# First mixer of a two-layer trunk: two groups of rotation tables, the state products, the gate weights and the head scales put elsewhere

## The chip, the cores and the metric

The kernel runs on one core of a Trainium2 chip. Its engines are TensorE (PE in the profile; its weight loads are PEld), VectorE (DVE), ScalarE (ACT), GpSimd (POOL) and SyncE (SP, which here issues the loads of weights). The metric is the device time of one execution in microseconds (us); lower is better. Three executions of the kernel before took 1027.24, 1029.93 and 1033.87 us, the median is 1029.93.

## The reference, cut to what matters

Two post-norm layers over 512 positions of width 1024; the even one mixes with HGRN2 heads and S5 groups, the odd one with two kinds of attention, and a mixture of 16 SwiGLU experts follows each. The change touches the even mixer alone:

```python
proj = jnp.einsum('bld,df->blf', x, ev_w_in[j])
q_a, f_a, i_a, g_a, u_b = split_cols(proj, [512, 512, 512, 512, 512])
# HGRN2: 4 heads of 128, chunks of 64 positions
f = lb + (1.0 - lb) * jax.nn.sigmoid(f_logit)
...                                    # b = cumsum(log f) in a chunk, decays exp(b), exp(-b)
o = o_intra + jnp.einsum('bhnck,bhnkv->bhncv', q_dec, S_prev)
o = o * lax.rsqrt(jnp.mean(o * o, axis=-1, keepdims=True) + RMS_EPS)
y_a = o * norm_g * jax.nn.silu(gate)
# S5: h_t = a h_{t-1} + B u_t, complex and diagonal, 32 groups of 16 inputs and 64 states
_, _, h_re, h_im = lax.associative_scan(combine, (a_re, a_im, drive_re, drive_im), axis=1)
y = jnp.einsum('blgp,gnp->blgn', h_re, c_re) - jnp.einsum('blgp,gnp->blgn', h_im, c_im)
y = jax.nn.gelu(y + d_skip * u)
z = jnp.einsum('blc,cf->blf', y, w_glu)
y_b = z[..., :512] * jax.nn.sigmoid(z[..., 512:])
mix = jnp.einsum('blf,fd->bld', jnp.concatenate([y_a, y_b], axis=-1), ev_w_out[j])
```

## The kernel before

Nothing is scheduled by a tool: every engine runs its instructions in the order in which the Python code emits them, and waits by semaphores for what it reads or overwrites. `weave(main, side)` interleaves generators: after each `yield` of the main one (a main step, 6 matmuls of 128x512) it lets the side one go on whose count has run out; a side generator that yields n sleeps for n main steps.

A product in full precision is three matmuls with operands split into a high and a low part (`mm3`, L198 to L200). The parts are made by `hilo`: L193 is the cast to the high part on ScalarE, L194 the subtraction that gives the low part on VectorE. Operands live in 13 buffers of 128x2048 (`unit`, named u), which are given out in turn, so a cast can also wait for the last reader of the buffer that it takes over. `tp`, `sd` and `acc` are PSUM tiles.

The first mixer in order of time:

- The projection of u (`tok(c["u"])`, L488). ScalarE copies the result into U (L485). `s5_tables` is woven in: cosines and sines of the rotation, Tc and Ts, built by doubling, eight groups of six VectorE operations (L861 to L866). The last two groups are the two halves of the last doubling.
- The projections of q, f and g as `main`, with four batches of the S5 scan (`s5_batches`) and `glu_prep` as `side`. One batch is: transposes of VT and U (L918, L924) with their ScalarE copies V and ut (L920, L926); products of EP and BB (L933) with ScalarE copies to MM (L938); GpSimd prepares VT and EP of the next batch (L879 to L903); sd from ut and V (L948); on VectorE the rotation of sd by Tc and Ts (L951 to L956), two scans (L958, L959) and the rotation back into H0 (L964) and H1 (L967); on TensorE the state products yp from MM, ut, EP and H (L972, L974); on VectorE their sum into U (L976). `YB` says after how many main steps each part of a batch goes on. `glu_prep` is the Gelu of U (L985, ScalarE) and, one per main step, four blocks fb of transposes (L992) with their `hilo`. Beside the last batch, `hgrn_f` does the gate's scan L540, the exponentials L544 and L545 (ScalarE) and their products L549 and L550 (VectorE) in two halves. The Silu of the g projection is L494. Sigmoid, log, exp, Gelu and Silu need different ScalarE tables; a change of table shows as ACT_TABLE_LOAD.
- `hgrn_main`, woven with the S5 gate product `glu()`: transposes L588, L590, state sums L614, L615, outputs L624, L628, and per block of 128 positions the sums of squares ms (L633). L581 multiplies the gate G by the norm weights ng, on GpSimd, once for all.
- `hgrn_out`, woven with the first half of the output product `wo_k`: the reciprocal roots scale the heads of V (L647), G multiplies them (L648), and L654 transposes the result.

Nothing after the mixer is touched. Line numbers are the profile's of the kernel before; in the changed kernel the same lines stand 2 to 5 further down (L194 is L196, L948 is L953, L974 is L979, L985 is L990).

## Time and profile before

| | us |
|---|---|
| three executions | 1027.24, 1029.93, 1033.87 |
| profiled execution, whole | 1029.0 |
| its span, first to last instruction | 1027.3 |
| PE busy | 852.1 (83%) |
| DVE busy | 789.2 (77%) |
| ACT busy | 562.3 (55%) |
| POOL busy | 308.3 (30%) |

The trace was taken from one execution; 1.7 us of its time lie outside the span. The first mixer ends at about 276 us of the span; the rest, 751 us, is the mixture of experts of the even layer, the odd layer and its mixture. Busy shares are means over stages that are bound by different things, so the time of a stage is read from what its waits end on. The mean granted clock of TensorE is given as a share of its full 2.4 GHz; 0.5 is the lower level, 1.2 GHz.

### The profile page before, as it was taken

How to read it: one execution, taken by the hardware profiler on the slowest of the kernel's cores; microseconds unless marked ns; L12 is line 12 of the kernel's file. 1: busy time of each engine (PE TensorE's matmuls, PEld its weight loads, DVE VectorE, ACT ScalarE, POOL GpSimd, SP SyncE). 2: the span in 40 equal slices, each digit the busy share in tenths (PEclk: the TensorE clock that was granted, in tenths of full speed). 3: DMA queues.
4: the chain of work that ended last, by engine and by line, in shares of the span. 5: the costliest groups of instructions: out<-in, count | busy, mean ns of one | idle time of the engine just before them, and what ended most of it. 6: DMA issues, size and time to landing. Idle time of an engine off the chain costs nothing.

```text
span 1027.3 us, 13161 instructions
## 1 busy us (share of the span) xinstructions
PE 852.1 (83%) x4396; PEld 713.6 (69%) x4396; DVE 789.2 (77%) x1542; ACT 562.3 (55%) x907; POOL 308.3 (30%) x343
## 2 busy tenths in 40 slices
PE   6968888889895789999885599989996689999830
PEld 5857777678784668888663488878785568888720
DVE  6996565656868879999777756888878869999647
ACT  3321334723402588998676245666712478999731
POOL 6357770210100222222221310245630222322203
PEclk9998999889997899999998699999998789999985
DMA  9312010301292879999893452060075869999822
GB/s 285 116 41 81 21 64 10 120 4 42 103 374 81 338 246 334 379 342 387 269 326 105 170 155 41 2 164 1 2 244 216 325 214 314 377 369 363 260 76 115
DMA packets 52875, 192.05 MB, mean 187 GB/s; under 512 B 13492, under 2 KB 15552, under 8 KB 38336
## 3 DMA queue, kind: packets, MB, share of 16 engines
q1 hardware_dynamic: 37344, 156.47, 41.8%
q0 software_dynamic: 13440, 24.17, 8.9%
q10 hardware_dynamic: 2016, 10.49, 2.6%
q8 instruction: 38, 0.62, 0.2%
q14 instruction: 37, 0.30, 0.1%
HBM read 183.20 MB, written 31.98 MB: 209 GB/s over the span
## 4 chain that ended last, share of the span: by engine, by line
PE 33%; issue 14%; DMA 13%; DVE 9%; POOL 5%; ACT 4%; SPq 1%; another core or an unknown queue 1%; ACTq 0%; POOLq 0%; DVEq 0%
DMA yd<-row,r 8%; PE acc L198 7%; PE acc L200 7%; PE acc L199 7%; DMA rx<-in_moe_w_gate_up_dram 2%; DVE u L194 2%; POOL yd L1612 2%; PE tp L207 2%; PE tp L1405 1%; DMA row<-yd 1%; ACT u L193 1%; POOL xg L1569 1%; DMA u<-in_moe_w_down_dram 1%; POOL row L1774 1%; PE sd L199 1%
## 5 line engine op out<-in xcount | busy, mean ns | idle before, releaser
L198 PE MATMUL acc<-u 128*128 128x512 f32 (+1 forms) x712 | 296.8, 417 | 9.9 <-ACT u L193 8.2
L200 PE MATMUL acc<-u 128*128 128x512 f32 (+1 forms) x712 | 282.3, 397 | 9.2 <-DVE u L194 9.2
L199 PE MATMUL acc<-u 128*128 128x512 f32 (+1 forms) x712 | 281.4, 395 | 3.0 <-POOL u L194 1.9
L194 DVE TENSOR_TENSOR u<-u 128x1024 fp32r<-128x1024 f32 x142 | 174.5, 1255 | 31.5 <-ACT u L193 30.3
L193 ACT CAST u<-u 128x1024 fp32r<-128x1024 f32 x150 | 152.7, 1050 | 68.9 <-PE acc L200 50.1
L194 DVE TENSOR_TENSOR u<-rx,u 128x1024 fp32r<-128x1024 f32 x128 | 152.3, 1220 | 29.6 <-ACT u L193 28.4
L200 PEld LDWEIGHTS acc<-u 128*128 128x128 f32 x712 | 141.3, 198 | 39.3 <-DVE u L194 12.2
L198 PEld LDWEIGHTS acc<-u 128*128 128x128 f32 x712 | 143.7, 202 | 33.4 <-ACT u L193 10.4
L199 PEld LDWEIGHTS acc<-u 128*128 128x128 f32 x712 | 142.5, 200 | 25.5 <-DVE u L194 3.5
L193 ACT CAST u<-rx 128x1024 fp32r<-128x1024 f32 x128 | 129.5, 1048 | 3.9 <-issue 1.3
L1612 POOL DMA_INDIRECT yd<-row,r x37 | 58.6, 1583 | 238.2 <-ACT row L1611 193.4
L193 ACT CAST u<-tp 128x512 fp32r<-128x512 f32 x102 | 60.1, 606 | 78.0 <-PE tp L207 67.1
L194 DVE TENSOR_TENSOR u<-tp,u 128x512 fp32r<-128x512 f32 x102 | 67.8, 698 | 19.0 <-ACT u L193 18.9
L1569 POOL DMA_INDIRECT xg<-x1d,r x41 | 47.3, 1153 | 77.0 <-PE tp L207 67.1
L207 PE MATMUL tp<-idf,xg 128*128 128x128 f32 x312 | 49.6, 299 | 16.4 <-DMA xg<-x1d,r 9.8
L207 PEld LDWEIGHTS tp<-idf,xg 128*128 128x128 f32 x312 | 46.7, 208 | 21.5 <-issue 10.0
L198 PE MATMUL acc<-u,ht 128*128 128x512 f32 x148 | 58.4, 395 | 4.0 <-ACT ht L193 4.0
L1395 POOL TENSOR_SCALAR P<-P,st 128x256 f32<-128x256 f32 (+3 forms) x32 | 35.0, 1094 | 87.5 <-DVE st L1371 52.3
L199 PE MATMUL acc<-u,ht 128*128 128x512 f32 x148 | 57.7, 390 | 0.0
L200 PE MATMUL acc<-u,ht 128*128 128x512 f32 x148 | 57.6, 389 | 0.0
L1611 ACT ACTIVATE row<-acc,r 128x512 f32<-128x512 f32 x74 | 47.7, 686 | 9.9 <-PE acc L200 9.9
L1113 ACT COPY u<-tp 128x512 f32<-128x512 f32 x16 | 9.4, 587 | 66.5 <-PE tp L1112 56.4
(394 smaller groups left out, 1443.5 us busy)
## 6 DMA issues: line engine op xcount, KB each, us to landing
rx<-in_moe_w_gate_up_dram SPq DMA_DIRECT2D x48, 1024.0 KB, 11.7
u<-in_moe_w_gate_up_dram SPq DMA_DIRECT2D x24, 1024.0 KB, 17.4
u<-in_moe_w_down_dram SPq DMA_DIRECT2D x19, 1024.0 KB, 15.4
rx<-in_moe_w_down_dram SPq DMA_DIRECT2D x16, 1024.0 KB, 13.2
u<-in_ev_w_in_dram SPq DMA_DIRECT2D x10, 1024.0 KB, 5.7
u<-in_ev_w_out_dram SPq DMA_DIRECT2D x4, 1024.0 KB, 4.9
x1d<-row POOLq DMA_DIRECT2D x8, 512.0 KB, 6.4
yd<-row ACTq DMA_DIRECT2D x8, 512.0 KB, 2.7
```

The source lines that it names most:

```text
L193: self.nc.scalar.copy(hi, src)
L194: (self.nc.gpsimd if pool else self.nc.vector).tensor_sub(lo, src, hi)
L198: nc.tensor.matmul(ps, ah, bh, start=start, stop=False)
L199: nc.tensor.matmul(ps, ah, bl, start=False, stop=False)
L200: nc.tensor.matmul(ps, al, bh, start=False, stop=stop)
L207: self.nc.tensor.transpose(tp[:, blk(j)], src[:, s], self.idf)
L1395: nc.gpsimd.tensor_scalar(P[:, 1, :W], P[:, 1, :W], st[:, 5, 1:2], None, op0=MUL)
L1405: nc.tensor.transpose(tp[:, blk(2 * b + x)], P[:, x, blk(b0 + b)], self.idf)
L1569: nc.gpsimd.indirect_dma_start(out=xg, out_offset=None, in_=self.x1d, in_offset=bass.IndirectOffsetOnAxis(ap=self.toki[:, s:s + 1], axis=0 ...
L1611: nc.scalar.activation(ys[:, blk(c, 512)], yp[c], AF.Copy, scale=self.gate[:, s:s + 1])
L1612: return lambda: self.scattered(s, nc.gpsimd.indirect_dma_start(out=self.yd, out_offset=bass.IndirectOffsetOnAxis(ap=self.toki[:, s:s + 1] ...
L1774: nc.gpsimd.tensor_mul(r[:, hi], r[:, hi], g[:, hi])
```

## The change

Four edits of the first mixer, all in the order or the engine of operations; the arithmetic is the same.

1. Of the eight groups of `s5_tables` six are woven into the projection of u, and the last two (12 VectorE operations) are emitted inside the first batch, after the preparation of the next batch and ahead of L948.
2. `YB` goes from 1, 2, 2, 3, 2 to 1, 2, 2, 5, 0: the state products stand two main steps later, and the next batch starts right behind them. The last batch yields 3 behind them, so that `glu_prep` comes later too.
3. L581, one GpSimd product of 128x2048, goes; `hgrn_main` multiplies G by ng in four VectorE operations of 128x512, each behind the sum of squares of its block.
4. L647, four VectorE products of 128x512, become 16 ScalarE copies of 128x128 with a scale per partition.

```diff
--- before.py
+++ after.py
@@ -1,4 +1,5 @@
 from contextlib import ExitStack
+from itertools import islice
 
 import concourse.bass as bass
 import concourse.tile as tile
@@ -32,9 +33,10 @@
 AHEAD = 6
 HGY = 7
 PSP = ()
-YB = 1, 2, 2, 3, 2
+YB = 1, 2, 2, 5, 0
 NTMP = 64
 NPREP = 8
+NTAB = 6
 NFIRST = 4
 SPT = 1
 PRE = 3
@@ -485,7 +487,8 @@
                 nc.scalar.copy(U[:, :, j].rearrange("c r g n -> c g r n"),
                                a.rearrange("c (g r n) -> c g r n", g=2, n=16))
             tabs = self.s5_tables()
-            weave(self.tok(c["u"], put_u, lambda j: slice(j, None, 4)), tabs)
+            early = islice(tabs, NTAB)
+            weave(self.tok(c["u"], put_u, lambda j: slice(j, None, 4)), early)
 
             def main():
                 yield from self.feat(c["q"], lambda j, a: nc.scalar.activation(Q[:, j, :], a, AF.Silu))
@@ -497,7 +500,7 @@
                 run_all(decay)
 
             def side():
-                yield from self.s5_batches(U)
+                yield from self.s5_batches(U, tabs)
                 yield from self.glu_prep(U)
             weave(main(), side())
             e5.close()
@@ -578,7 +581,6 @@
             z = hg.tile([128, 128], F32, name=f"S{h}", bufs=3)
             nc.gpsimd.memset(z, 0.0)
             S.append(z)
-        nc.gpsimd.tensor_mul(G, G, ng.unsqueeze(1).to_broadcast([128, NT, 512]))
         ms = self.ms = hg.tile([128, NT, 4], F32, name="ms")
 
         def front(tt):
@@ -631,6 +633,7 @@
             sq = hg.tile([128, 512], F32, name="sq", bufs=2)
             nc.scalar.activation(sq, po, AF.Square)
             nc.vector.reduce_sum(ms[:, tt, :], sq.rearrange("p (h v) -> p h v", h=4), axis=AX.X)
+            nc.vector.tensor_mul(G[:, tt, :], G[:, tt, :], ng)
             yield 1
 
     def hgrn_out_prep(self, O):
@@ -643,8 +646,8 @@
     def hgrn_out(self, O, G):
         nc = self.nc
         for tt in range(NT):
-            o4 = O[:, tt, :].rearrange("p (h v) -> p h v", h=4)
-            nc.vector.tensor_mul(o4, o4, self.rsm[:, tt, :].unsqueeze(2).to_broadcast([128, 4, 128]))
+            for h in range(4):
+                nc.scalar.activation(O[:, tt, blk(h)], O[:, tt, blk(h)], AF.Copy, scale=self.rsm[:, tt, h:h + 1])
             nc.vector.tensor_mul(O[:, tt, :], O[:, tt, :], G[:, tt, :])
         self.dump("ya", O)
         yield HGY
@@ -902,7 +905,7 @@
             G.tensor_tensor(EP[0][sl, :, 1:5, g, :], t1[sl], t2[sl], op=SUB)
             G.tensor_scalar(EP[1][sl, :, 1:5, g, :], u1[sl], -1.0, None, op0=MUL)
 
-    def s5_batches(self, U):
+    def s5_batches(self, U, tabs):
         nc, s5, I = self.nc, self.s5, self.I
         Vv = nc.vector
         big = lambda nm: s5.tile([128, 4, 128], F32, name=nm)
@@ -910,7 +913,6 @@
         f2 = lambda a: a.rearrange("p r c -> p (r c)")
         for q in range(4):
             ps, EP = slice(4 * q, 4 * q + 4), self.EPs[q % 2]
-            Tc, Ts = self.Tc[:, ps], self.Ts[:, ps]
             Vm = []
             for i in range(2):
                 tp = self.tp()
@@ -939,6 +941,9 @@
             if q < 3:
                 self.s5_inputs(q + 1)
                 self.s5_outputs(q + 1)
+
+            run_all(tabs)
+            Tc, Ts = self.Tc[:, ps], self.Ts[:, ps]
             yield YB[0]
 
             dps = []
@@ -974,7 +979,7 @@
                     nc.tensor.matmul(o, self.H[i][:, r, :], EP[i][:, r, 1:5].rearrange("p k g n -> p (k g n)"),
                                      start=False, stop=i == 1)
             Vv.tensor_add(Y[:, ps], Y[:, ps], yp.rearrange("c (r l f) -> c r l f", r=4, l=4))
-            yield YB[4]
+            yield YB[4] if q < 3 else 3
         self.Y = Y
 
     def glu_prep(self, U):
```

The order on VectorE around the end of the projection of u, before. L863 to L866 are the last table operations; u there are the tables Tc and Ts, p the rotations that they are doubled by, g scratch.

```order
L863 TENSOR_TENSOR u<-g_808,g_809 128x16x32
L864 TENSOR_TENSOR g_808<-u,p_202 128x512
L865 TENSOR_TENSOR g_809<-u,p_201 128x512
L866 TENSOR_TENSOR u<-g_808,g_809 128x16x32
L194 TENSOR_TENSOR u<-u 128x1024 x3
L951 TENSOR_TENSOR g_1063<-sd,u 128x512
L952 TENSOR_TENSOR h_1065<-sd,u 128x512
```

In the changed kernel the three splits of q's first operands stand behind the sixth group:

```order
L867 TENSOR_TENSOR g_808<-u,p_200 128x512
L868 TENSOR_TENSOR g_809<-u,p_199 128x512
L869 TENSOR_TENSOR u<-g_808,g_809 128x16x32
L196 TENSOR_TENSOR u<-u 128x1024 x3
L864 TENSOR_TENSOR g_808<-u,p_201 128x512
L865 TENSOR_TENSOR g_809<-u,p_202 128x512
```

and the last operations ahead of the first batch's rotation are these:

```order
L866 TENSOR_TENSOR u<-g_808,g_809 128x16x32
L867 TENSOR_TENSOR g_808<-u,p_202 128x512
L868 TENSOR_TENSOR g_809<-u,p_201 128x512
L869 TENSOR_TENSOR u<-g_808,g_809 128x16x32
L956 TENSOR_TENSOR g_1063<-sd,u 128x512
L957 TENSOR_TENSOR h_1065<-sd,u 128x512
```

So the three L194 moved ahead of the last two groups, and these stand between them and L956, which is L951 before.

TensorE between the state products of the first batch and the second batch, before. L198 to L200 are the main steps' matmuls, of which 42 stand between L948 and the first L972, and 12 between the last L974 and L918:

```order
L972 MATMUL sd<-MM,ut 128x128
L974 MATMUL sd<-EP_147,H_155 128x128
L974 MATMUL sd<-EP_148,H_156 128x128
L198 MATMUL acc<-u 128x512
L199 MATMUL acc<-u 128x512
L200 MATMUL acc<-u 128x512
```

and now, with 54 matmuls between L953 and the first L977:

```order
L977 MATMUL sd<-MM,ut 128x128
L979 MATMUL sd<-EP_147,H_155 128x128
L979 MATMUL sd<-EP_148,H_156 128x128
L920 MATMUL tp<-idf,VT_151 128x128 x4
L920 MATMUL tp<-idf,VT_152 128x128 x4
L926 MATMUL tp<-idf,U 128x128 x4
```

The two main steps that stood behind the state products stand ahead of them, and the transposes of the next batch follow at once.

ScalarE from the first exponentials to the first Silu, before (L193 with tp is the high part of a Gelu block fb):

```order
L544 ACT_TABLE_LOAD
L544 ACTIVATE u<-u 128x1024
L545 ACTIVATE u<-u 128x1024
L193 CAST u<-u 128x1024
L985 ACT_TABLE_LOAD
L985 ACTIVATE u<-U 128x16x2x16 x4
L544 ACT_TABLE_LOAD
L544 ACTIVATE u<-u 128x1024
L545 ACTIVATE u<-u 128x1024
L193 CAST u<-tp 128x4x128 x2
L193 CAST u<-u 128x1024
L494 ACT_TABLE_LOAD
```

and now:

```order
L547 ACT_TABLE_LOAD
L547 ACTIVATE u<-u 128x1024
L548 ACTIVATE u<-u 128x1024
L195 CAST u<-u 128x1024
L547 ACTIVATE u<-u 128x1024
L548 ACTIVATE u<-u 128x1024
L990 ACT_TABLE_LOAD
L990 ACTIVATE u<-U 128x16x2x16 x4
L195 CAST u<-u 128x1024
L497 ACT_TABLE_LOAD
L497 ACTIVATE G<-acc 128x512 x2
L195 CAST u<-tp 128x4x128
```

The second pair of exponentials moved ahead of the Gelu, with one table load less, and the casts of the Gelu's blocks now stand between the Silus of G (two of the four ahead of the first cast).

## Rows read from the trace of the kernel before

**Rows 1.** Stages by window: us; PE, PEld, DVE, ACT, POOL busy; clock; DMA.

```profile
60.00:104.00 44.00, 31.36 (x153) 26.71 (x153) 32.26 (x39) 9.37 (x15) 24.02 (x33) 0.88 0.21 71
104.00:158.20 54.20, 47.78 (x258) 40.84 (x257) 32.31 (x35) 17.94 (x27) 40.87 (x54) 0.94 0.12 40
158.20:210.90 52.70, 41.58 (x200) 33.12 (x199) 35.22 (x40) 29.87 (x37) 12.37 (x19) 0.89 0.19 65
210.90:276.00 65.10, 60.97 (x371) 51.32 (x370) 42.17 (x110) 23.57 (x36) 1.87 (x3) 0.98 0.07 20
```

**Rows 2.** Timeline of PE, batches 0 to 3: start, length, idle before in brackets.

```profile
65.81 0.50 PE L198 MATMUL acc<-u 128*128 128x512 f32 x1 [1.62 <-ACT U L485]
...
76.58 1.12 PE L924 MATMUL tp<-idf,U 128*128 128x128 f32 x4 [8.24 <-ACT V L920]
...
97.23 0.73 PE L974 MATMUL sd<-EP,H 128*128 128x128 f32 x2 [2.16 <-DVE H L967]
...
101.11 0.48 PE L198 MATMUL acc<-u 128*128 128x512 f32 x1
...
103.94 1.04 PE L918 MATMUL tp<-idf,VT 128*128 128x128 f32 x8
...
158.19 1.03 PE L918 MATMUL tp<-idf,VT 128*128 128x128 f32 x8
...
165.16 0.48 PE L198 MATMUL acc<-u 128*128 128x512 f32 x1
```

**Rows 3.** The window of batch 0's state products, columns as in rows 1.

```profile
94.00:101.20 7.20, 4.46 (x23) 4.27 (x24) 4.24 (x5) 0.00 (x0) 2.89 (x3) 0.76 0.23 61
```

**Rows 4.** Timeline of DVE: tables, splits, chains of batches 0 and 1.

```profile
60.84 0.77 DVE L861 TENSOR_TENSOR g<-u,p 128x512 f32<-128x512 f32 x1
...
65.65 0.69 DVE L861 TENSOR_TENSOR g<-u,p 128x512 f32<-128x512 f32 x1
...
69.75 0.69 DVE L861 TENSOR_TENSOR g<-u,p 128x512 f32<-128x512 f32 x1
...
73.74 3.55 DVE L194 TENSOR_TENSOR u<-u 128x1024 fp32r<-128x1024 f32 x3
...
83.34 0.69 DVE L951 TENSOR_TENSOR g<-sd,u 128x512 f32<-128x512 f32 x1 [6.05 <-PE sd L948]
...
96.41 0.77 DVE L967 TENSOR_TENSOR H<-g,g 128x508 f32<-128x508 f32 x1
...
123.60 0.69 DVE L967 TENSOR_TENSOR H<-g,g 128x508 f32<-128x508 f32 x1
```

**Rows 5.** Timeline of ACT: the cast ahead of batch 0's copies.

```profile
74.99 1.05 ACT L193 CAST u<-u 128x1024 fp32r<-128x1024 f32 x1 [7.77 <-DVE u L194]
```

**Rows 6.** Timeline of ACT behind the Gelu.

```profile
189.41 1.28 ACT L544 ACT_TABLE_LOAD   x1
...
192.76 1.96 ACT L193 CAST u<-tp 128x512 fp32r<-128x512 f32 x2
...
198.37 1.04 ACT L193 CAST u<-u 128x1024 fp32r<-128x1024 f32 x1 [3.65 <-PE tp L992]
```

**Rows 7.** Timeline of DVE: the last split of the S5 gate's weights.

```profile
205.54 4.70 DVE L194 TENSOR_TENSOR u<-u 128x1024 fp32r<-128x1024 f32 x1 [0.76 <-ACT u L193]
```

**Rows 8.** Timeline of POOL: the gate product.

```profile
204.65 4.51 POOL L581 TENSOR_TENSOR G<-G,ng 128x2048 f32<-128x2048 f32 x1 [6.28 <-ACT G L494]
```

**Rows 9.** Timeline of PE: the last wait ahead of L588.

```profile
210.30 0.79 PE L200 MATMUL acc<-u 128*128 128x512 f32 x1 [4.01 <-DVE u L194]
```

**Rows 10.** Timeline of DVE at the end of the mixer.

```profile
262.00 3.49 DVE L194 TENSOR_TENSOR u<-u 128x1024 fp32r<-128x1024 f32 x3
...
270.79 1.22 DVE L194 TENSOR_TENSOR u<-u 128x1024 fp32r<-128x1024 f32 x1
```

**Rows 11.** Timeline of PE at the end of the mixer.

```profile
272.66 1.25 PE L654 MATMUL tp<-idf,V 128*128 128x128 f32 x8 [2.98 <-DVE u L194]
```

**Rows 12.** Groups by shape, ACT: a later stage's 128x128; xcount | busy, mean ns.

```profile
L1381 ACT ACTIVATE P<-acc,st 128x128 f32<-128x128 f32 x16 | 5.7, 366 | 3.5 <-DVE st L1375 1.6 <-DVE st L1373 1.5 <-DVE st L1372 0.4
```

## Prediction

> **What bounds the kernel now.** I read the windows by stage first, then the timelines of the engines that wait there. In the four stages that the change touches [rows 1], 60 to 276 us, TensorE is busy 31.4 of 44.0, 47.8 of 54.2, 41.6 of 52.7 and 61.0 of 65.1 us; so up to 34 us of the mixer are TensorE's waiting, while VectorE has room in each (32 of 44, 32 of 54, 35 of 53, 42 of 65). Everything behind the mixer is the same code, waits for the mixer's end and should shift as a block.
>
> Where TensorE waits [rows 2]: 1.62 us for the copies into U and 8.24 us for the copies of V (at 65.81 and 76.58), then for H1 behind the scan (2.16 us at 97.23). The 8.24 us come from ScalarE: its queue stands at a cast that takes over a buffer whose last reader is L194 [rows 5], and L194 stands on VectorE behind the last two groups of tables, from 65.65 to 73.74 [rows 4]. Nothing of batch 0 needs these tables before L951, and VectorE then idles 6.05 us for L948 [rows 4]. The state products of batch 0 run at a granted clock of 0.76 as the mean of their window [rows 3], so partly at the lower level, 1.2 GHz, after the waits on H. Batches 1 and 2 repeat the wait on H; from L918 to L918 they take (158.19 - 103.94)/2 = 27.1 us each [rows 2]. Ahead of the HGRN stage TensorE waits 4.01 us [rows 9] for a split that took 4.70 us [rows 7] while GpSimd ran L581 [rows 8]; the same split takes 3.55/3 = 1.2 us elsewhere [rows 4].
>
> **Term A, to L918 of batch 1.** Rates first. The twelve main matmuls between 101.11 and 103.94 took 2.83 us [rows 2]: 0.236 us each, and 54 of them 12.7 us. From L918 to the end of L948 batch 3 took 165.16 - 158.19 = 7.0 us [rows 2], with no long wait in it. In the changed order the cast ahead of U's copies takes a buffer that is read earlier, so the 1.62 us go, and L918 starts at 67.3 - 1.6 = 65.7; L948 ends at 72.7, the 54 matmuls at 85.4. VectorE: three splits from 65.65 to 69.2, then the two late groups. A group took 69.75 - 65.65 = 4.10 us with GpSimd idle and 65.65 - 60.84 = 4.81 us with GpSimd at work [rows 4]. GpSimd starts the next batch's preparation some 2 us behind L918, so I take 4.81: the tables end at 78.8 (77.4 by the other). The chain from L951 to the end of L967 took 97.18 - 83.34 = 13.8 us [rows 4], beside GpSimd all the way: H1 stands at 92.6. VectorE is then the bound of batch 0, and TensorE waits some 7 us at the state products. From H1 to the next main matmul it took 101.11 - 97.23 = 3.9 us [rows 2], at the low clock; after so long a wait I keep that: L918 of batch 1 at 96.5 instead of 103.94. A = 7.4. With the short table time, a chain one us shorter (GpSimd ends before it does) and the full clock it would be 11; with everything 1.5 us longer, 6.
>
> **Term B, batches 1 and 2.** H1 of batch 1 ended at 123.60 + 0.69 = 124.29 [rows 4], 20.35 us behind its L918, a time that VectorE's own chain sets. Two more main steps ahead of the state products fill the wait: 7.0 + 12.7 = 19.7, then 0.6 us of wait. One such wait is shorter than each that now stands there (2.16 in batch 0), so I take the full clock for what follows, half of 3.9, 2.0 us. The next L918 comes at 20.35 + 2.0 = 22.4 instead of 27.1 us: 4.7 us per batch, B = 9.4. If the clock falls all the same it is 24.3, and B = 5.6; if waits inside the chain shrink too, 10. GpSimd needs about 20 us of such a batch (40.9 us in two batches [rows 1]), so it fits in 22.4, with little to spare.
>
> **Term C, batch 3 to L588.** Before: 210.9 - 158.2 = 52.7 us [rows 1]. The Gelu was done at 189.41 [rows 6], 31.2 us behind L918. In the new order the second pair of exponentials runs ahead of it: 192.76 - 189.41 - 1.28 = 2.1 us [rows 6], its table load left out. The Gelu ends at 33.3. TensorE is at 22.4 behind the state products and has 30 matmuls, 7.1 us, until the first Gelu block: 29.5, so a new wait of up to 3.8 us there. Behind the Gelu ScalarE's queue sets the pace: before, it took from 198.37 [rows 6] to 205.54 [rows 7], 7.2 us, for two casts of weights, a table load, four Silus and two casts of blocks; now there are four casts of blocks, 1.96 us more [rows 6]: 33.3 + 9.1 = 42.4. Then the last split, 1.2 us, since L581 is gone, and the last matmuls: L588 at about 43.8. C = 52.7 - 43.8 = 8.9. If the chain of batch 3 comes later, or the casts wait for TensorE's transposes, which wait for the splits of the blocks ahead, C falls to 5.5; with the faster ends it is 10.5.
>
> **Term D, the end of the mixer.** Four products of G by ng, 0.69 us each (the 128x512 products of [rows 4]), come to VectorE. Three stand in a stage where VectorE idles 22.9 of 65.1 us [rows 1], behind the sums of squares, where it waits for TensorE; should that cover be gone, they cost 2.1 us. The fourth stands ahead of the roots: 0.7 us on the path. Off the path come the four L647: the eight products took from 262.00 + 3.49 to 270.79, 5.3 us [rows 10]. ScalarE's 16 scales are bounded by 128x128 activations of 0.366 us [rows 12], 5.9 us in all, from about 262.7 to 268.6; the last L648 ends at 269.3, where before it ended at 270.8. The second L654, which waited till 272.66 [rows 11], comes 1 to 2 us earlier: D = 1.3.
>
> **The sum.** 7.4 + 9.4 + 8.9 + 1.3 = 27.0 us. The profiled execution took 1029.0, the median is 1029.9, so the two bases differ by 0.9; 1002.0 on the one, 1002.9 on the other. I say 1002.
>
> **Rivals.** One: TensorE stays low. After each wait on H the state products run at 1.2 GHz as now, in batches 1 and 2 too (B = 5.6), and batch 3 loses to its queues (C = 5.5, A = 6, D = 1): 18 us, 1011. For it speaks that rows 3 show the clock low after 2.2 us of waiting; against it, that the waits get shorter in batches 1 and 2.
>
> Two: GpSimd and VectorE shut each other out. The late tables have been put beside GpSimd's preparation of batch 1. If each of the 12 operations had to let one GpSimd operation through, with a mean of 24.02/33 = 0.73 us [rows 1], they would take 12 x (0.69 + 0.73) = 17.0 us, not 9.6; H1 comes 7.4 us later, A is nothing, and the time is 1009.5. The split of 4.70 us beside L581's 4.51 [rows 7, 8] speaks for it, the group of 4.81 us beside a busy GpSimd [rows 4] against it. The Trainium skill, page "SBUF — State Buffer", section "Who interferes with whom", has this as a rule: a VectorE operation with two inputs in SBUF and a GpSimd operation that reads SBUF share a port pair, and the second one blocks fully until the first is done. By that rule the late tables are put in the worse of two places; the trace agrees for the one long GpSimd operation and shows a sixth more time, not a double one, for many short ones.
>
> Three: the gain is not kept. The stages after the mixer, or the longer ScalarE queue, give most of it back: the mixer's end is then no path, and the time is 1020 to 1030. Against it: nothing that follows starts before the mixer's output.
>
> Four, slower: the low clock outlasts a wait. TensorE now waits some 7 us at H of batch 0 and 3.8 us at the Gelu. If the granted clock fell at the Gelu and stayed at 1.2 GHz in the HGRN stage, its 61.0 us of matmuls [rows 1] would take up to 61 us more; from 27 us more, 45% of them, the change is slower, with all of them it is 1063, at two thirds 1043. Against it: the low stretch of [rows 3] ended within 4 us of steady matmuls, and the stage now runs at 0.98.
>
> **How the numbers follow.** The forecast (994 to 1008): 0.68. TensorE low, 1011: 0.13. Shut out, 1009.5: 0.10. Not kept: 0.06. Slower: 0.03. About 1%, 10 us, is what a measurement of this kernel can tell from no change. The first three rivals of the list split so that all of the first two and the forecast are faster by more than that, 0.91; the third lies within it, 0.06; the last is slower, 0.03. The fast ends of the terms (11, 10, 10.5, 2) sum to 33.5, 996, and the executions before lie up to 4 us from their median, so the low end is 994; the high end takes in rivals one and two, 1012.
>
> **What would show it.** In the changed profile: L918 of batch 0 at 65 to 66 with no wait over 1 us to its L948; VectorE without a break from the splits to H1 at 91 to 94; a TensorE wait for H1 of 5 to 8 us in batch 0 and under 1 us in batches 1 and 2; L918 every 22 to 23 us at full clock; a wait of 3 to 4 us at the Gelu's first block, no split of weights over 1.5 us, L588 some 44 us behind batch 3's L918; the second L654 without its 2.98 us; the stage from 276 on as long as before. I am wrong if VectorE's chain grows beyond 14 us, if the clock stays low through whole batches, or if the last stage changes.

## The result, and the profile after

The changed kernel took 1005.46 us as the median of 4 executions (1002.60 to 1008.00); beside it the kernel before took 1031.05 (1027.24 to 1033.87). The ratio is 0.974, with an interval from 0.9705 to 0.9776. A later set of executions of the same two kernels gave 0.971 (0.9685 to 0.9735). Predicted were 1002 and a range from 994 to 1012. The profiled execution has a span of 1001.9 us, 25.4 less than before.

The stages by window, cut at the first transposes of batches 1 and 3, at L590 (L588 before) and at the mixer's end; the columns are those of [rows 1]:

```profile
60.00:97.70 37.70, 29.44 (x153) 25.61 (x152) 34.45 (x39) 8.74 (x14) 31.12 (x33) 0.91 0.20 65
97.70:143.25 45.55, 44.00 (x258) 37.62 (x258) 32.74 (x35) 18.44 (x28) 41.49 (x54) 1.00 0.18 63
143.25:187.20 43.95, 39.32 (x200) 31.29 (x199) 32.78 (x41) 28.15 (x35) 8.62 (x19) 0.96 0.24 78
187.20:252.30 65.10, 62.50 (x383) 52.29 (x383) 44.49 (x112) 29.76 (x53) 3.65 (x4) 1.00 0.11 35
```

TensorE waited some 34 us in [rows 1]; now it is idle 8.3, 1.6, 4.6 and 2.6 us, 17 in all, and half of that is in batch 0. The rows of TensorE that answer to [rows 2, 9, 11]:

```profile
66.75 0.66 PE L926 MATMUL tp<-idf,U 128*128 128x128 f32 x4 [0.24 <-ACT V L922]
...
91.30 0.79 PE L979 MATMUL sd<-EP,H 128*128 128x128 f32 x2 [6.17 <-DVE H L969]
...
93.95 0.80 PE L979 MATMUL sd<-EP,H 128*128 128x128 f32 x2 [1.86 <-DVE H L972]
...
97.74 1.04 PE L920 MATMUL tp<-idf,VT 128*128 128x128 f32 x8
...
118.16 0.49 PE L979 MATMUL sd<-EP,H 128*128 128x128 f32 x2 [0.48 <-DVE H L972]
...
120.50 1.04 PE L920 MATMUL tp<-idf,VT 128*128 128x128 f32 x8
...
174.52 0.33 PE L997 MATMUL tp<-idf,u 128*128 128x128 f32 x1 [1.40 <-ACT u L990]
...
186.98 0.50 PE L202 MATMUL acc<-u 128*128 128x512 f32 x1 [0.63 <-DVE u L196]
...
187.32 0.60 PE L590 MATMUL tp<-idf,F 128*128 128x128 f32 x4
...
246.37 1.25 PE L657 MATMUL tp<-idf,V 128*128 128x128 f32 x8 [0.96 <-DVE u L196]
```

The 8.24 us for the copies of V are 0.24 us now. Where TensorE waited twice for H in every batch it waits once, 0.48 us, in batches 1 and 2, and L920 comes every 22.76 us (120.50 - 97.74) instead of 27.1. In batch 0 the wait grew to 6.17 and 1.86 us. The 4.01 us ahead of L588 and the 2.98 us at the second transposes of the end are 0.63 and 0.96.

The granted clock of TensorE, ahead of the state products of batch 0, through them and behind them, and last behind the Gelu's first block (columns as above):

```profile
84.70:90.50 5.80, 0.44 (x3) 0.21 (x2) 5.80 (x6) 0.00 (x0) 5.76 (x6) 0.97 0.00 0
90.50:97.70 7.20, 4.54 (x22) 4.25 (x23) 4.46 (x6) 0.00 (x0) 3.09 (x4) 0.55 0.20 46
97.70:117.00 19.30, 19.00 (x106) 16.04 (x106) 13.31 (x15) 10.04 (x15) 16.88 (x24) 1.00 0.10 39
176.21:178.91 2.70, 2.70 (x7) 2.02 (x8) 2.07 (x4) 2.67 (x4) 2.17 (x7) 0.50 0.00 0
```

Through the state products of batch 0 it is 0.55, so mostly the lower level of 1.2 GHz; through batches 1 and 2 it is full (1.00 from 97.70 to 143.25). Behind the Gelu's first block it is at the lower level again for 2.7 us: six main matmuls start 0.42 to 0.57 us apart there, where those ahead of the Gelu start 0.23 apart. VectorE, the rows that answer to [rows 4, 7]:

```profile
65.63 4.55 DVE L196 TENSOR_TENSOR u<-u 128x1024 fp32r<-128x1024 f32 x3
...
70.11 1.09 DVE L864 TENSOR_TENSOR g<-u,p 128x512 f32<-128x512 f32 x1
...
80.83 0.69 DVE L956 TENSOR_TENSOR g<-sd,u 128x512 f32<-128x512 f32 x1
...
93.13 0.77 DVE L972 TENSOR_TENSOR H<-g,g 128x508 f32<-128x508 f32 x1
...
185.72 1.21 DVE L196 TENSOR_TENSOR u<-u 128x1024 fp32r<-128x1024 f32 x1
```

It works without a break from the splits to H1 at 93.90, and each part is longer or shorter than it was: the three splits 4.5 us (3.55 before), the two late groups 80.83 - 70.11 = 10.7 (8.1), the chain 13.1 (13.8). ScalarE, around the Gelu and at the end:

```profile
173.83 2.19 ACT L990 ACTIVATE u<-U 128x512 f32<-128x512 f32 x4
...
237.84 4.80 ACT L650 ACTIVATE V<-V,rqy 128x128 f32<-128x128 f32 x16 [0.91 <-DVE rqy L281]
```

The Gelu ends at 176.0, 32.8 us behind L920 of batch 3; the sixteen scales take 4.80 us, one every 0.30.

From the same marks in both traces the four terms are:

| term | marks | before | after | gain | predicted |
|---|---|---|---|---|---|
| A | start of batch 1's first transposes | 103.94 | 97.74 | 6.2 | 7.4 |
| B | from there to those of batch 3 | 54.25 | 45.51 | 8.7 | 9.4 |
| C | from there to L588 | 52.70 | 44.07 | 8.6 | 8.9 |
| D | from there to the second L654 | 61.77 | 59.05 | 2.7 | 1.3 |
| rest | from there to the end of the span | 754.6 | 755.5 | -0.9 | 0 |

They sum to 25.4, the difference of the spans.

### The profile page after: what moved, and what is told of

It is laid out like the page before. It is cut to its first block, busy times and chain, and to the rows that moved or that the text cites. A ratio compares the mean times of both kernels' runs of the same rounds, so it can differ in the third digit from the quotient of the medians.

```text
span 1001.9 us, 13169 instructions
## 1 busy us (share of the span) xinstructions
PE 845.2 (84%) x4396; PEld 707.5 (71%) x4396; DVE 789.1 (79%) x1542; ACT 566.4 (57%) x922; POOL 311.9 (31%) x342
## 3 DMA queue, kind: packets, MB, share of 16 engines
q1 hardware_dynamic: 37344, 156.47, 42.5%
## 4 chain that ended last, share of the span: by engine, by line
PE 47%; issue 15%; DVE 14%; DMA 12%; ACT 5%; POOL 5%; another core or an unknown queue 1%; ACTq 0%; SPq 0%; POOLq 0%; DVEq 0%
PE acc L200 10%; PE acc L202 10%; PE acc L201 10%; DMA yd<-row,r 8%; PE tp L209 2%; DVE u L196 2%; POOL yd L1617 2%; ACT u L195 1%; DMA xg<-x1d,r 1%; PE tp L1410 1%; POOL xg L1574 1%; DMA row<-yd 1%; PE sd L201 1%; PE sd L200 1%; POOL row L1779 1%
## 5 line engine op out<-in xcount | busy, mean ns | idle before, releaser
L200 PE MATMUL acc<-u 128*128 128x512 f32 (+1 forms) x712 | 296.5, 416 | 6.9 <-ACT u L195 6.9
L196 DVE TENSOR_TENSOR u<-u 128x1024 fp32r<-128x1024 f32 x142 | 172.2, 1241 | 27.0 <-ACT u L195 25.9
L195 ACT CAST u<-u 128x1024 fp32r<-128x1024 f32 x150 | 152.9, 1051 | 41.4 <-PE acc L202 36.6
L196 DVE TENSOR_TENSOR u<-rx,u 128x1024 fp32r<-128x1024 f32 x128 | 152.3, 1220 | 28.9 <-ACT u L195 27.8
L200 PEld LDWEIGHTS acc<-u 128*128 128x128 f32 x712 | 143.8, 202 | 29.9 <-ACT u L195 8.7
L200 PE MATMUL acc<-u,ht 128*128 128x512 f32 x148 | 58.5, 395 | 4.0 <-ACT ht L195 4.0
```

The source lines that it names most:

```text
L195: self.nc.scalar.copy(hi, src)
L196: (self.nc.gpsimd if pool else self.nc.vector).tensor_sub(lo, src, hi)
L200: nc.tensor.matmul(ps, ah, bh, start=start, stop=False)
```

## The experiments

Theory: TensorE's waits for the scan are what the mixer lost, the new places of the state products take most of them away, and what is left in batch 0 is VectorE's chain, stretched by GpSimd beside it. Rivals: the late tables or the gate product carry the gain; the wait in batch 0 comes from something else.

All kernels below but one are compared with the kernel before on the same chip. In the table b0, b1, b2 are the times from one batch's first transposes to the next one's, C and D those above; b0 has no part of the 1.62 us wait ahead of the first transposes, which only the kernel before and u_tabs have.

| kernel | ratio to before | interval | b0 | b1 | b2 | C | D |
|---|---|---|---|---|---|---|---|
| before | 1 | | 36.6 | 27.1 | 27.1 | 52.7 | 61.8 |
| changed | 0.974 | 0.9705 to 0.9776 | 32.3 | 22.8 | 22.8 | 44.1 | 59.1 |
| changed, again (base5) | 0.971 | 0.9685 to 0.9735 | 33.0 | 23.1 | 22.8 | 44.1 | 59.0 |
| u_tabs | 0.976 | 0.9722 to 0.9798 | 32.0 | 22.8 | 22.8 | 44.1 | 59.1 |
| u_yb | 0.9903 | 0.9874 to 0.9931 | 35.0 | 27.1 | 27.1 | 49.5 | 60.1 |
| u_gate | 0.9751 | 0.9718 to 0.9784 | 32.2 | 22.8 | 22.7 | 45.1 | 58.6 |
| u_scale | 0.9777 | 0.9737 to 0.9817 | 32.9 | 23.2 | 22.8 | 44.1 | 61.0 |
| a_tabs | 0.9987 | 0.9962 to 1.0011 | 36.1 | 27.1 | 25.5 | 53.5 | 62.7 |
| x_hold | 0.9736 | 0.9701 to 0.9772 | 31.8 | 22.8 | 22.8 | 44.1 | 59.0 |
| v_qtab | 0.9695 | 0.9651 to 0.9739 | 24.8 | 23.1 | 23.1 | 44.1 | 59.1 |
| v_qtab5, the same kernel | 0.9642 | 0.9617 to 0.9667 | 26.0 | 23.3 | 23.1 | 44.1 | 59.0 |
| v_qhold | 0.9662 | 0.963 to 0.9695 | 24.5 | 24.0 | 23.1 | 44.1 | 59.1 |
| v_act | 0.9712 | 0.9684 to 0.9741 | 25.1 | 23.4 | 23.3 | 44.5 | 59.0 |

The changed kernel stands in the table twice, and its own b0 and b1 differ by 0.8 and 0.3 us between two executions: a stage's time from one trace tells about a microsecond there. C and D repeat to 0.1 us wherever an edit leaves them alone.

### The tables: undone (u_tabs) and alone (a_tabs)

```diff
-NTAB = 6
+NTAB = 8
```

> The changed kernel with all eight groups of tables early again (NTAB 8), the rest kept. Theory, both edits work on the same wait of batch 0: the copies of V come late again, and L920 of batch 0 to L953 shifts by some 11 us, but the 54 matmuls and the chain to H1 then end nearly together (H1 at 97 as in the kernel before), so L920 of batch 1 comes at 99.4 instead of 97.7 and the whole is 1.5 to 2.5 us above the changed kernel, 1006 to 1008. Rival, the terms of the prediction add up: term A (6.2 us measured) belongs to the tables, and the time is 1011 to 1012.

Measured: 1006.07 us, ratio 0.976, so about 2 us above the changed kernel's 0.974, with intervals that overlap: the timing alone can't tell the two apart. TensorE's timeline in u_tabs:

```profile
64.70 0.50 PE L200 MATMUL acc<-u 128*128 128x512 f32 x1 [1.62 <-ACT U L487]
...
75.51 1.12 PE L926 MATMUL tp<-idf,U 128*128 128x128 f32 x4 [8.28 <-ACT V L922]
...
95.84 0.49 PE L979 MATMUL sd<-EP,H 128*128 128x128 f32 x2 [0.40 <-DVE H L972]
```

The old waits of 1.62 and 8.28 us are back, but the state products then find H1 after 0.40 us. This trace is already 1.1 us ahead at the first of these waits (64.70, where [rows 2] have 65.81), so the starts of batch 1 can't be compared as they stand. Counted with the wait, b0 takes 31.97 + 1.62 = 33.59 us here and 32.26 in the changed kernel: the late tables are worth 1.3 us (0.6 against base5's b0), under the theory's 1.5 to 2.5. As the theory had it, late tables and later state products spend themselves on one wait.

The other way round, the kernel before with the tables alone:

```diff
+NTAB = 6
-weave(self.tok(c["u"], put_u, lambda j: slice(j, None, 4)), tabs)
+weave(self.tok(c["u"], put_u, lambda j: slice(j, None, 4)), islice(tabs, NTAB))
...
+            run_all(tabs)
+            Tc, Ts = self.Tc[:, ps], self.Ts[:, ps]
             yield YB[0]
```

> The kernel before with the late tables alone. Theory: L918 of batch 0 at 65.5, H1 at 93.9 as in the changed kernel, L918 of batch 1 twelve matmuls behind the state products at 100.5 instead of 103.9; all else as before: 3.4 us below the kernel before. With the run with all tables early this shows whether the gains of the two edits add: alone 3.4, on top of the new YB some 2. Rival, they add: 6 us below.

Measured: 1029.43 us, ratio 0.9987 (0.9962 to 1.0011): no gain that the timing can tell, and the expected 3.4 us lie just inside the interval. In the trace b0 is 0.5 us shorter, and the 1.62 us ahead of it are gone: 2.1 us, less than expected. TensorE's timeline in a_tabs:

```profile
89.16 0.80 PE L978 MATMUL sd<-EP,H 128*128 128x128 f32 x2 [7.96 <-DVE H L968]
...
91.81 0.79 PE L978 MATMUL sd<-EP,H 128*128 128x128 f32 x2 [1.85 <-DVE H L971]
```

The wait for V's copies became a wait for H: 7.96 + 1.85 us, where the kernel before waits 0.62 and 2.16 there. VectorE is the bound of batch 0 either way. Batch 2 is 1.6 us shorter here than in the kernel before (25.5 and 27.1), which the tables don't explain: its waits for H are 1.31 and 1.63 us, much as there (1.26 and 1.63), but the clock stayed at 1.00 behind them (window 147.00 to 149.30), where the kernel before has 0.56 (151.45 to 155.33). C and D are 0.8 and 0.9 us longer, so nothing of this shows in the whole.

### The later state products undone (u_yb)

```diff
-YB = 1, 2, 2, 5, 0
+YB = 1, 2, 2, 3, 2
...
-            yield YB[4] if q < 3 else 3
+            yield YB[4]
```

> The changed kernel with the old YB (1, 2, 2, 3, 2), so state products two main steps earlier, Gelu ahead of the second exponentials; late tables, gate weights and scales as in the changed kernel. Theory: batches 1 and 2 take 27.1 us each again (8.7 in all), L920 of batch 1 comes at 100.5 (2.8 more), batch 3 to L590 takes 49 to 50 instead of 44 (the 4.7 us split stays short): 16 to 18 us above the changed kernel, 1021 to 1023. Rival, the late tables and the gate weights carry the gain: under 8 us above.

Measured: 1020.85 us, ratio 0.9903. That is 16.8 us above the changed kernel's ratio (0.0163 of 1031), as expected. TensorE's timeline in u_yb:

```profile
117.53 0.49 PE L979 MATMUL sd<-EP,H 128*128 128x128 f32 x2 [1.29 <-DVE H L969]
...
119.64 0.79 PE L979 MATMUL sd<-EP,H 128*128 128x128 f32 x2 [1.63 <-DVE H L972]
...
202.39 0.79 PE L202 MATMUL acc<-u 128*128 128x512 f32 x1 [0.43 <-DVE u L196]
```

The two waits for H of 1.29 and 1.63 us are back, and so are the 27.1 us. By stages: b0 2.8, b1 and b2 8.8, C 5.4, D 1.0 us. So one of the change's four edits, the new YB with the order of the Gelu that comes with it, carries most of the gain; the rival falls. What the later state products and the later Gelu are worth each, no run separates.

### The gate product and the head scales undone (u_gate, u_scale)

```diff
+        nc.gpsimd.tensor_mul(G, G, ng.unsqueeze(1).to_broadcast([128, NT, 512]))
...
-            nc.vector.tensor_mul(G[:, tt, :], G[:, tt, :], ng)
```

> The changed kernel with the gate product on GpSimd again (L581 of the kernel before), the four VectorE products by ng taken out. Theory: L581 starts behind the last Silu of G, beside the last splits of the Gelu blocks and of the S5 gate's weights; the last split takes 4 to 5 us again, TensorE waits 3 to 4 us ahead of L590 and its first transposes run at the low clock; the mixer's end gains 0.7 us back: 3 to 4.5 us above the changed kernel. Rival, ScalarE's queue sets L590 and the split is hidden: under 1 us.

Measured: 1006.32 us, ratio 0.9751, about 1 us above the changed kernel and not told apart from it. The expectation was wrong. The timelines of GpSimd, VectorE and TensorE in u_gate around the last split:

```profile
181.49 4.61 POOL L584 TENSOR_TENSOR G<-G,ng 128x2048 f32<-128x2048 f32 x1 [3.83 <-ACT G L497]
```

```profile
185.00 2.18 DVE L196 TENSOR_TENSOR u<-u 128x1024 fp32r<-128x1024 f32 x1
```

```profile
187.24 0.50 PE L202 MATMUL acc<-u 128*128 128x512 f32 x1 [1.58 <-DVE u L196]
```

The product takes 4.61 us, much as before (4.51), but the last split beside it 2.18 and not 4.70: in the new order most of the product is over when the last split comes; they overlap for 1.1 us (185.00 to 186.10), where [rows 7, 8] show 3.6 (205.54 to 209.16). In both kernels the split ends 1.08 us behind the product's end (187.18 - 186.10 and 210.24 - 209.16), and by itself it takes 1.2: so it got next to nothing done while the product ran. TensorE waits 1.58 us instead of 0.63, C is 1.0 us longer and D 0.5 us shorter. In the old order the same product costs much more: u_yb, without it, waits 0.43 us ahead of its L590, and a_tabs, with it, this by its timeline of TensorE:

```profile
204.94 0.79 PE L202 MATMUL acc<-u 128*128 128x512 f32 x1 [4.01 <-DVE u L196]
```

So what the product cost was a matter of where it stood, and the new order had moved the splits away from it before it was taken out.

```diff
-            for h in range(4):
-                nc.scalar.activation(O[:, tt, blk(h)], O[:, tt, blk(h)], AF.Copy, scale=self.rsm[:, tt, h:h + 1])
+            o4 = O[:, tt, :].rearrange("p (h v) -> p h v", h=4)
+            nc.vector.tensor_mul(o4, o4, self.rsm[:, tt, :].unsqueeze(2).to_broadcast([128, 4, 128]))
```

> The changed kernel with the head scales on VectorE again (four products of 128x512 instead of 16 ScalarE copies). Theory: eight products behind the three splits instead of four, so the second group of transposes at the mixer's end comes 1 to 2 us later. Rival, that end is set by ScalarE's casts of the transposed blocks: no difference, under 0.3 us.

Measured: 1008.01 us, ratio 0.9777, some 4 us above the changed kernel with overlapping intervals; in the trace D is 61.01 - 59.05 = 1.96 us longer. TensorE's timeline at the second transposes of the end in u_scale:

```profile
247.78 1.71 PE L657 MATMUL tp<-idf,V 128*128 128x128 f32 x8 [2.93 <-DVE u L196]
```

The wait of 2.93 us is that of [rows 11], 2.98. The theory holds, at its upper end.

### GpSimd beside VectorE (x_hold, x_noprep)

```diff
             run_all(tabs)
+            if q == 0:
+                nc.gpsimd.tensor_copy(s5.tile([128, 4], F32, name="hold"), self.Ts[:, 0:4, 127])
             if q < 3:
                 self.s5_inputs(q + 1)
                 self.s5_outputs(q + 1)
```

> The changed kernel with one small GpSimd copy of a column of the finished table Ts ahead of the preparation of batch 1, so that GpSimd starts it behind the late tables instead of beside them. Theory, contention with GpSimd stretched the splits and the late tables (4.55 and 10.7 us): they take 3.6 to 4.2 and 8.2 to 8.6 us, the chain to H1 13 to 14 us as it is, H1 comes 2 to 3 us earlier and L920 of batch 1 too: 2 to 3 us below the changed kernel. Rival, the operations are slow for another reason (the clock of the engine, waits on each other): 10.7 us still, and GpSimd late with EP for batch 1: 0 to 4 us above.

Measured: 1003.53 us, ratio 0.9736; not told apart from the changed kernel. VectorE, from the first late table operation to L956 (L958 here) to H1:

```profile
68.43 1.09 DVE L864 TENSOR_TENSOR g<-u,p 128x512 f32<-128x512 f32 x1
...
77.12 0.69 DVE L958 TENSOR_TENSOR g<-sd,u 128x512 f32<-128x512 f32 x1
...
90.49 1.09 DVE L974 TENSOR_TENSOR H<-g,g 128x508 f32<-128x508 f32 x1
```

The tables take 8.7 us instead of 10.7, nearly the 8.2 to 8.6 expected, but the splits still take 4.5 and the chain takes 14.5 instead of 13.1: H1 comes 27.8 us behind the first transposes instead of 28.4. So GpSimd's preparation cost VectorE much the same time wherever the two met. The expectation failed in the splits, which run beside two GpSimd operations that stand ahead of the held one, and in the chain, which it took as full of contention already.

```diff
-            if q < 3:
+            if 0 < q < 3:
                 self.s5_inputs(q + 1)
                 self.s5_outputs(q + 1)
...
-            ps, EP = slice(4 * q, 4 * q + 4), self.EPs[q % 2]
+            ps, EP = slice(4 * q, 4 * q + 4), self.EPs[0 if q == 1 else q % 2]
```

> The changed kernel with GpSimd's preparation of batch 1 left out (batch 1 works with batch 0's VT and EP; batch 2's preparation stays). It asks only what VectorE takes in batch 0 without GpSimd beside it. Theory, contention is the whole stretch and holding GpSimd back only moved it: tables 8.2 to 8.4 us, the chain from L956 to H1 11 to 11.5 us instead of 13.1, H1 some 22.5 to 23.5 us behind L920 of batch 0 instead of 28.4 (the first splits, which run beside the two GpSimd operations that stay, still 4.5). Rival, holding gained little because the chain of batch 0 is slow by itself: H1 at 26 or later.

Measured in one execution, read for batch 0 alone; its whole time of 1009.84 us says nothing on the question, since batch 1 then waits for GpSimd's EP (b1 27.8 us). VectorE's timeline in x_noprep, the same three places:

```profile
69.43 1.09 DVE L864 TENSOR_TENSOR g<-u,p 128x512 f32<-128x512 f32 x1
...
78.11 0.69 DVE L956 TENSOR_TENSOR g<-sd,u 128x512 f32<-128x512 f32 x1
...
88.31 0.69 DVE L972 TENSOR_TENSOR H<-g,g 128x508 f32<-128x508 f32 x1
```

Tables 8.7 us (the first of them still beside the two GpSimd operations that stay), chain 10.9, H1 24.2 us behind the first transposes at 64.83: 4.2 us earlier than in the changed kernel. The parts came within 0.3 us of what was expected; the sum in the expectation was too low by a slip (its own parts give 23.7 to 24.4, not 22.5 to 23.5), and 24.2 is well under the rival's 26. So of the 28.4 us that VectorE takes to H1, 4.2 are GpSimd's preparation, and the other 24.2 are VectorE's own work but for the 1 us by which the two GpSimd operations that stay stretch the splits (4.5 us, 3.55 in [rows 4]). Holding GpSimd back could not bring much, and less work for VectorE ahead of H1 could.

### A version that beats both: the last doubling cut by batches (v_qtab, v_qtab5)

Batch q uses four of the sixteen rows of Tc and Ts. So the last doubling can be done for these rows in each batch, where VectorE idles some 5.4 us ahead of L956 in batches 1 to 3:

```diff
             run_all(tabs)
+            self.s5_last(q)
...
+    def s5_last(self, q):
+        ps, o, n_ = slice(4 * q, 4 * q + 4), slice(0, 64), slice(64, 128)
+        cb, sb = [e[:, ps].unsqueeze(2).to_broadcast([128, 4, 64]) for e in self.e[6]]
+        ...                                  # the six operations of a group, 128x256 each
```

> The changed kernel with the last doubling of the tables (12 operations of 128x512) cut into the four rows of each batch: 6 operations of 128x256 in each batch, where the 12 stood in batch 0. The same values. Theory, batch 0 is bound by VectorE and batches 1 to 3 have VectorE idle for some 5.4 us ahead of L956: H1 of batch 0 at 87 to 89 instead of 93.9, L920 of batch 1 at 90 to 92 instead of 97.7; batches 1 and 2 lose up to 1.5 us each because GpSimd, slowed by the new operations beside it, hands over EP with 0.8 us to spare now: 3 to 7 us below the changed kernel, 998 to 1002. Rival, the wait at batch 0 is set by the clock or by GpSimd: no gain.

Measured: 998.39 us, ratio 0.9695. TensorE's timeline in v_qtab, the state products of batches 0 and 1:

```profile
87.27 0.49 PE L995 MATMUL sd<-EP,H 128*128 128x128 f32 x2 [2.17 <-DVE H L988]
...
110.41 0.49 PE L995 MATMUL sd<-EP,H 128*128 128x128 f32 x2 [0.88 <-DVE H L988]
```

The wait of batch 0 fell from 6.17 + 1.86 to 0.18 + 2.17 us, b0 from 32.3 to 24.8 us; b1 and b2 lost 0.3 to 0.4 us each, to a wait for H1 of 0.9 instead of 0.5 us, and not to GpSimd's EP. Both kernels once more, on one chip:

> The kernel with the last doubling cut by batches once more, beside the changed kernel on the same chip: 6 to 7 us below it, as its trace gave (mixer shorter by 6.8 us from L920 of batch 0 to the end). Rival, the stages behind give a part of it back: 3 us or less.

> The changed kernel itself on the same chip as the three before: 0.974 of the kernel before, 25 to 28 us below it.

Measured: 996.34 us, ratio 0.9642 (0.9617 to 0.9667), and the changed kernel 1002.81, ratio 0.971 (0.9685 to 0.9735). The changed kernel is 30 us below the kernel before here, where 25 to 28 were expected. The intervals don't touch: 6.5 us less than the changed kernel, so nearly all of the 6.8 us that the mixer's trace gave arrives at the end.

### Two additions to it (v_qhold, v_act)

```diff
             self.s5_last(q)
+            if q == 0:
+                nc.gpsimd.tensor_copy(s5.tile([128, 4], F32, name="hold"), self.Ts[:, 0:4, 127])
```

> The kernel with the last doubling cut by batches, and GpSimd held back in batch 0 until that batch's part of the tables is done. Theory: splits and the six operations of batch 0 take 2 us less, TensorE's wait for H1 in batch 0 goes from 2.2 to under 0.6 us: 1 to 2 us below the kernel with the cut alone, 996.5 to 997.5 if that takes 998.4. Rival, GpSimd then hands EP of batch 1 over too late (17.4 us from 71 on, wanted at some 89.5) and runs beside the whole chain: no gain or up to 2 us above.

Measured: 997.17 us, ratio 0.9662, not told apart from v_qtab. The rival came true; TensorE's timeline in v_qhold:

```profile
86.03 0.49 PE L997 MATMUL sd<-EP,H 128*128 128x128 f32 x2 [2.32 <-DVE H L990]
...
91.66 1.72 PE L950 MATMUL tp<-EP,BB 128*32 128x128 f32 x14 [0.58 <-POOL EP L921]
```

The wait for H1 is still 2.32 us, and the products of EP now wait 0.58 us for GpSimd.

```diff
-                G.tensor_copy(self.VT[i][sl, :, 3, g, :], self.Bb[i][sl, 4 * q:4 * q + 4, :])
+                (nc.scalar.copy if q else G.tensor_copy)(self.VT[i][sl, :, 3, g, :], self.Bb[i][sl, 4 * q:4 * q + 4, :])
...
-            G.tensor_copy(EP[0][sl, :, 0, g, :], self.C[0][sl, 4 * q:4 * q + 4, :])
-            G.tensor_scalar(EP[1][sl, :, 0, g, :], self.C[1][sl, 4 * q:4 * q + 4, :], -1.0, None, op0=MUL)
+            nc.scalar.copy(...), nc.scalar.mul(...)         # for q > 0, ahead of the power products
```

> The kernel with the last doubling cut by batches, and the plain copies of VT and EP for batches 1 to 3 (8 operations per batch of 64x64 elements, that need no power products) moved from GpSimd to ScalarE. Theory, every GpSimd operation with an input in SBUF stretches VectorE's chain beside it: H1 comes 0.6 to 0.9 us earlier per batch, the waits of 2.2, 0.9 and 0.8 us shrink to 1.4, 0.3 and 0.3: 1 to 2 us below the kernel with the cut alone. Rival, the 128x256 products are what hurts and the copies lie beside nothing: within 0.5 us.

Measured: 1004.00 us, ratio 0.9712: 7.7 us above v_qtab5 on the same chip, where a gain of 1 to 2 or nothing was expected. Neither theory foresaw it. The mixer is not the place: from the first transposes of batch 0 to the second group of the end it takes 239.85 - 64.50 = 175.4 us, in the two traces of v_qtab 174.1 and 175.5. The loss lies behind it. TensorE at the first gathered rows of the mixture of experts, in v_act and in v_qtab5, by their timelines:

```profile
306.81 1.95 PE L209 MATMUL tp<-idf,xg 128*128 128x128 f32 x8 [8.23 <-DMA xg<-x1d,r]
```

```profile
302.38 1.95 PE L209 MATMUL tp<-idf,xg 128*128 128x128 f32 x8 [4.90 <-DMA xg<-x1d,r]
```

Counted from the second transposes of the mixer's end this is 67.0 and 63.6 us: 3.3 of 7.1 us by which the rest of the span is longer (763.95 and 756.84) are lost at a transfer, the gather from x1d. GpSimd begins it only 0.3 us later in v_act (at 300.09, 60.2 us behind those transposes; at 298.74, 60.0 us, in v_qtab5), so the loss is in the gather itself: its first rows reach TensorE 6.7 us behind its start instead of 3.6. But the eight copies are not shown to be the cause: x_noprep, which has none of them, waits 8.20 us for the same gather, and every other trace 4.73 to 4.91. Most of the other 3.8 us come in the second mixture: from its last products of the routing tile r to its last gathered rows it takes 168.5 us in v_act, 165.4 in v_qtab5, and 169.0 in a_tabs, again without the copies. So v_act is slower by more than its interval, and why stays open.

## Why the prediction was right, and where its terms were off

**Term A** was 7.4 and came as 6.2. L918 at 65.7 (65.48), L948's end and the bound by VectorE came as written; the step that was mis-sized is VectorE's time to H1, 92.6 predicted and 93.90 measured. The three splits were taken at 3.5 us and took 4.5, the late groups at 9.6 and took 10.7, the chain at 13.8 and took 13.1: GpSimd's work lay beside all three. x_noprep, in one execution, shows that the stretch is GpSimd's and what it is worth, 4.2 us; x_hold that shifting the preparation did not dodge it. What the term did not say is whose gain it is: it was worked out for tables and state products together, and u_tabs and a_tabs show that they share one wait, so that the tables add only some 1 us in the new surroundings and 2 in the old.

**Term B**, 9.4, came as 8.7: the wait for H1 was 0.48 us (0.6 predicted), and the full clock behind it held, with 120.50 - 118.16 = 2.3 us to the next transposes instead of the 2.0 taken. It is the term that u_yb gives back whole. Of each batch's 4.4 us some 1.5 are clock: the state products behind the last wait took 3.88 us at 0.56 before (151.45 to 155.33) and 2.34 at 1.00 now (118.16 to 120.50). The reason given for it, a wait shorter than each that stood there, is hardly so beside the 0.62 us of batch 0 before, and the length of the wait does not settle the clock: in a_tabs the clock stayed full once behind the old waits, and it fell in batch 0 of one execution of v_qtab's kernel behind the same wait that left it full in another (last section). So the full clock in both batches was not certain.

**Term C**, 8.9, came as 8.6, with two errors inside that the sum hides. The wait at the Gelu was taken as up to 3.8 us; TensorE stood there idle for 1.40 and twice 0.19 us, and took 3.1 us from its arrival to the end of the block (173.12 to 176.21), since the Gelu ended 0.5 us earlier than worked out and the first quarters could be transposed while the others ran. Left out was the clock behind it, 0.50 for 2.7 us; it cost TensorE some 1.3 us there (six matmuls in 2.70 us instead of 1.4), covered by ScalarE's queue, which worked without a gap from 175.93 to 183.31. And the short split was put down to L581's going; u_gate shows that the new order alone had brought it from 4.70 to 2.18 us, and that L581 itself was worth 1.0 us there, of which the four products that replace it take 0.5 back in D. The pace of ScalarE's queue behind the Gelu, 9.1 us and a split, came as written: 185.72 is 42.5 us behind L920 of batch 3, 42.4 predicted.

**Term D**, 1.3, came as 2.7. The scales are worth 1.96 us by u_scale, where some 1.5 were worked out (270.8 - 269.3): ScalarE's scales last 0.388 us each but start 0.30 apart, so that the sixteen took 4.80 us and not 5.9, and VectorE's last product by G is done at 243.62, ahead of the first transposes of the end (244.37). The four gate products cost 0.5 us by u_gate. The missing 1.2 us is clock. The same transposes and products from L588 to the next main matmul, in the kernel before and in the changed one:

```profile
210.89:213.30 2.41, 2.41 (x13) 2.41 (x12) 0.00 (x0) 1.16 (x2) 0.00 (x0) 0.50 0.00 0
```

```profile
187.32:188.56 1.24, 1.24 (x13) 1.24 (x12) 0.00 (x0) 0.56 (x1) 0.00 (x0) 1.00 0.00 0
```

The wait ahead of them is 0.63 and not 4.01 us now; the prediction counted that wait and forgot what the clock did after it. Here too that one wait does not settle the clock: u_yb waits 0.43 us there and has 0.58 (202.98 to 205.40), u_gate waits 1.58 and has 1.00 (187.57 to 188.81).

**The sum.** 27.0 us were predicted and 25.4 measured. It is nearer than its terms: A and B together came 1.9 us short and D 1.4 over, for reasons that have nothing to do with each other. That part is luck.

**The rivals.** TensorE staying low: not in batches 1 and 2; the low stretches are batch 0's state products, 0.55 in their window, and 2.7 us behind the Gelu. GpSimd and VectorE shutting each other out: the twelve late operations would have taken 17.0 us and took 10.7, with 8.2 beside an idle GpSimd, so 0.3 of the way. Not kept: the rest of the span moved by 0.9 us in the profiled pair and lies between 754.6 and 764.1 us in all traces of this study, so this spread, and not the mixer, limits what a timing tells. Slower by a clock that stays low: no; it did fall at the Gelu, but the HGRN stage ran at 1.00, where it was 0.98.

The page that the prediction weighed, the Trainium skill's "SBUF — State Buffer", section "Who interferes with whom", says that a VectorE instruction with two SBUF inputs contends with a GpSimd instruction that reads SBUF, and calls what they share an exclusive lock. For one long GpSimd product the traces agree: VectorE's split ended 1.08 us behind the product's end whether the two overlapped for 3.6 or for 1.1 us. For many short operations the rule, taken as rival two took it, made the price too high: 10.7 us were measured, not 17.0.

## What to carry to other kernels

Two edits that shorten the same wait don't add: before counting both, ask what the wait becomes when either is there alone. When an engine in order is the bound of one stage and idle in the next ones, look for work in front of the bound that only the later stages need, and cut it by what each uses: that gave 6.5 us here, where moving the whole block gave 1 to 2. The contention between two engines moved with the work here (x_hold, v_qhold); what shortened the stage was less work on one of them (x_noprep, v_qtab).

## What the runs showed of the hardware

A VectorE operation with both inputs in SBUF stood still beside a long GpSimd product that reads SBUF: the split of 128x1024, 1.2 us by itself, took 4.70 us in the kernel before, 4.71 in a_tabs and 2.18 in u_gate, and each time it ended 1.08 to 1.09 us behind the product's end.

The VectorE operations here with an input in PSUM show no such stretch. In the changed kernel the four products of batch 0's rotation that read sd, from PSUM, took 0.68 to 0.69 us each beside GpSimd's preparation, as without it in x_noprep; the two sums behind them, with both inputs in SBUF, took 0.95 and 1.22 us, in x_noprep 0.68 and 0.69.

VectorE's 128x512 operations with two inputs and GpSimd's 128x192 products, both on SBUF, fell nearly into step where they met. In the changed kernel, by the timelines of VectorE and of GpSimd:

```profile
72.15 0.89 DVE L866 TENSOR_TENSOR u<-g,g 128x512 f32<-128x512 f32 x1
...
73.07 0.89 DVE L867 TENSOR_TENSOR g<-u,p 128x512 f32<-128x512 f32 x1
```

```profile
72.45 0.96 POOL L882 TENSOR_TENSOR bim<-cnre,pw 128x192 f32<-128x192 f32 x1
...
73.37 0.96 POOL L882 TENSOR_TENSOR pt<-cnim,pw 128x192 f32<-128x192 f32 x1
```

Each starts 0.92 us after its last. Around this pair GpSimd's four products start 0.91 to 0.92 us apart and VectorE's operations 0.81 to 1.03. VectorE's take 0.69 us beside an idle GpSimd [rows 4], and GpSimd's 0.51 beside an idle VectorE, by the timeline of GpSimd in the kernel before:

```profile
80.11 0.51 POOL L879 TENSOR_TENSOR bre<-cnim,pw 128x192 f32<-128x192 f32 x1
```

The step is longer than either and shorter than the sum of 1.20. So neither waited for the other's whole length as the profile has it; whether they take turns within the step, the traces don't show.

The clock after one and the same wait is not the same in every execution. In batch 0 of the kernel cut by batches the state products follow waits of 0.18 and 2.17 us in v_qtab and of 0.25 and 2.17 us in v_qtab5, and the clock is 1.00 up to their end. From there to the next transposes, in v_qtab and in v_qtab5:

```profile
87.27:89.61 2.34, 2.34 (x21) 2.34 (x22) 1.12 (x1) 0.00 (x0) 2.19 (x3) 1.00 0.09 12
```

```profile
85.80:89.27 3.47, 3.47 (x20) 3.47 (x21) 1.11 (x1) 0.00 (x0) 2.48 (x3) 0.65 0.33 71
```

The same matmuls take 2.3 us in one and 3.5 in the other. Behind the single waits of 0.48 to 0.59 us it stayed full in batches 1 to 3 of the changed kernel.
